# The last stage of a streaming encoder step: where its weights and residual are fetched, and in which order its blocks, sums and outputs run

## The chip, the core and the metric

The kernel runs on one core of a Trainium2 chip. A core has TensorE (PE, matrix products into PSUM), VectorE (DVE), ScalarE (ACT), GpSimd (POOL) and SyncE (SP, whose queue issues the DMAs). The metric is the device time of one execution in microseconds (us), the median of several runs.

## The reference, cut to what matters

An encoder trunk of two layers works on 656 tokens of 1024 channels (16 meta tokens, 512 prompt tokens, 8 x 16 sample tokens), all in float32. In each layer a mixing block adds to the residual, then a gated feed-forward block does; after the second layer the result is normalised. The end of the second layer is what the change touches:

```python
    gate, val = jnp.split(h2 @ p['w_up'].astype(x.dtype), 2, axis=-1)
    gate_c, ffn_new = causal_dwconv(gate, ffn_past, p['ffn_conv_w'], p['ffn_conv_b'])
    x = x + (jax.nn.gelu(gate_c) * val) @ p['w_down'].astype(x.dtype)
...
    y_prompt = rmsnorm(xp, g_final)[:, N_META:]
    y_sample = rmsnorm(xs, g_final)
```

w_up is 1024 x 5632 and w_down 2816 x 1024. The 2816 inner channels are 22 blocks of 128; the 1024 model channels are 8 blocks of 128, called m = 0 to 7 below.

## The kernel before, in words

Channels lie on the 128 partitions and tokens along the free dimension. Every float32 product is made from three matrix products in a reduced format: an operand is split into a high part (a cast on ScalarE) and a low part (operand minus high part, on VectorE), and `mm3` adds high x high, high x low and low x high into the same PSUM tile. So a block of weights can be used when its load (`w_load`, a tile "raw"; there are 4 of them), its cast (`ghi` or `whi`) and its subtraction (`glo` or `wlo`) are done. `weights` issues the three one after another; with its last argument true the two parts go to tiles of the large pool of 57 slots, else to a small pool of 4.

**The feed-forward stage.** The products with w_up are made for pairs of inner blocks by a scheme of seven products (`strassen`), 12 matrix instructions each. One pair takes seven products for its gate and seven for its value; 133 such products run in the last layer, numbered by `nprod`. When a pair is done, its gated values are multiplied on GpSimd (`gv`, L1275 and L1277), and `val_split` splits them into `hi_g` and `lo_g` (L332, L333), the moving operand of the products with w_down. The inner blocks are taken in four parts (`PARTS`: 6, 6, 6 and 4 blocks). The products of the first three parts with w_down run between the seven-product groups (`down`, named `d_dn`): their results are added by GpSimd-issued DMAs onto the residual, which lies in DRAM (`x_scr`, L1306). The list `steps` holds this order; L1340 opens a block in which VectorE and TensorE follow it as written, while the tile scheduler orders ScalarE, GpSimd and the DMA queues. Splits of finished values wait in the list `later`, which gives one up after each product; what is left is emptied at L1361.

**The last stage** (from L1373) does the fourth part, inner blocks 18 to 21, for the last layer. It stands behind that block, so the scheduler orders all engines. The 640 tokens that matter are cut into two chunks, `CF`: 384 and 256 tokens wide. For each chunk it goes over m = 0 to 7: 4 inner blocks x 3 = 12 matrix instructions into one PSUM tile (`d_fin`); VectorE adds the residual block `x` (L1386), which `x_in` has fetched from `x_scr` (L424); ScalarE squares the sum (`sq`, L408) and scales it (`y`, L1390); GpSimd adds the squares up, for m = 7 VectorE (L413). Then `norm_r` sums the squares over the partitions with a matrix product by ones (`np_fin`, L312), takes the root's reciprocal on ScalarE (L313, L314) and refines it on VectorE (L315, L317); each `y` is multiplied by it (L1394; GpSimd for m = 1 and 4, VectorE for the others) and stored. The weights of m = 0 and 1 are fetched ahead of the loop (`WA` = 2), those of m + 2 and the residual of m within the pass m of the first chunk. PSUM has 8 tiles: 3 in one pool (`PD`) and 5 in another (`PB`); `PX` goes round over both.

## Time and profile before

| | us |
|---|---|
| median of 3 runs (lowest to highest) | 1698.6 (1696.43 to 1701.21) |
| the profiled execution: its time | 1697.38 |
| the profiled execution: its span, first to last instruction | 1695.6 |
| PE busy in the span | 1625.4 (96%) |
| DVE busy | 1238.9 (73%) |
| ACT busy | 878.7 (52%) |
| POOL busy | 581.7 (34%) |

The span lies 1.78 us under the time of the same execution. Stretches are given in us from the span's start. The granted clock of TensorE is a share of full speed: it has two levels, 2.4 GHz (1.00) and 1.2 GHz (0.50), and a value between them is a mean over a stretch.

### The profile page before, as it was taken

What the parts mean: (1) busy time and instruction counts of PE and PEld (TensorE: products, weight loads), DVE (VectorE), ACT (ScalarE), POOL (GpSimd) and SP (SyncE); (2) the same over time, 40 slices, a digit from 0 to 9 for tenths busy, and PEclk for the clock granted to TensorE, in tenths of its full rate; (3) what the DMA queues carried; (4) which work ended last, traced back from release to release, by engine and by line L of the source; (5) the groups of instructions that cost most, each with busy time, mean ns of one, the idle gap of its engine ahead of it and who ended that gap; (6) DMA issues with size and microseconds to landing.
All of it is one profiled execution on the core that took longest, in us unless ns stands there. A gap on an engine that the chain in (4) does not pass through costs nothing.

```text
span 1695.6 us, 28745 instructions
## 1 busy us (share of the span) xinstructions
PE 1625.4 (96%) x10772; PEld 1532.0 (90%) x10772; DVE 1238.9 (73%) x2380; ACT 878.7 (52%) x1744; POOL 581.7 (34%) x668
## 2 busy tenths in 40 slices
PE   7999999998999999999999999999999999999985
PEld 6898888898899999999998978789888999999984
DVE  6579985769877767766648898776898767776444
ACT  5656576553545444444445647575454444444343
POOL 0102220008466554553001122100476555554423
PEclk9999999999999999999999999999999999999998
DMA  5236431342145344444612555214411344344442
GB/s 205 90 96 159 115 99 36 112 154 79 50 112 119 100 105 106 102 102 107 221 65 89 128 130 122 67 65 136 144 38 60 95 120 107 101 102 98 119 110 94
DMA packets 75003, 180.56 MB, mean 106 GB/s; under 512 B 12752, under 2 KB 18384, under 8 KB 74864
## 3 DMA queue, kind: packets, MB, share of 16 engines
q1 hardware_dynamic: 62192, 149.36, 27.3%
q0 software_dynamic: 12672, 29.37, 11.1%
q8 instruction: 84, 1.38, 0.3%
q14 instruction: 55, 0.45, 0.1%
HBM read 129.80 MB, written 35.46 MB: 97 GB/s over the span
## 4 chain that ended last, share of the span: by engine, by line
PE 78%; DVE 10%; issue 4%; POOL 3%; ACT 2%; DMA 2%; SPq 0%; DVEq 0%; POOLq 0%; ACTq 0%
PE d_i L374 16%; PE d_dn L374 15%; PE d_v L374 12%; PE d_g L374 12%; PE d_oa L374 5%; PE e_i L374 2%; PE sc L491 2%; DMA x<-x_scr 1%; PE hl L785 1%; PE po L527 1%; PE e_u L374 1%; DVE fh L1066 1%; DVE wlo L361 1%; PE d_ob L374 1%; DVE wlo L968 1%
## 5 line engine op out<-in xcount | busy, mean ns | idle before, releaser
L374 PE MATMUL d_v<-fh,whi 128*128 128x328 f32 (+1 forms) x1120 | 251.6, 312 | 1.4 <-ACT whi L967 1.4
L360 ACT CAST whi<-raw 128x384 fp32r<-128x384 f32 (+2 forms) x243 | 132.5, 548 | 210.1 <-PE d_i L374 75.5
L374 PE MATMUL d_g<-fh,whi 128*128 128x328 f32 (+1 forms) x1008 | 226.5, 312 | 0.3 <-ACT whi L967 0.3
L374 PE MATMUL d_i<-hi_h,whi 128*128 128x328 f32 x672 | 219.0, 326 | 0.0
L374 PE MATMUL d_i<-lo_h,whi 128*128 128x328 f32 x672 | 213.8, 318 | 0.0
L374 PE MATMUL d_i<-hi_h,wlo 128*128 128x328 f32 x672 | 212.8, 317 | 0.0
L374 PE MATMUL d_dn<-hi_g,wlo 128*128 128x328 f32 (+1 forms) x640 | 199.9, 312 | 2.8 <-DVE wlo L361 2.8
L374 PE MATMUL d_dn<-hi_g,whi 128*128 128x328 f32 (+1 forms) x640 | 200.2, 313 | 1.9 <-ACT hi_g L332 1.7
L374 PE MATMUL d_dn<-lo_g,whi 128*128 128x328 f32 (+1 forms) x640 | 200.2, 313 | 1.8 <-DVE lo_g L333 1.8
L361 DVE TENSOR_TENSOR wlo<-raw,whi 128x384 fp32r<-128x384 f32 (+2 forms) x243 | 169.7, 713 | 30.4 <-ACT whi L360 20.5
L374 PEld LDWEIGHTS d_v<-fh,whi 128*128 128x128 f32 x1120 | 189.3, 189 | 1.6 <-ACT whi L967 1.6
L968 DVE TENSOR_TENSOR wlo<-wcb,whi 128x512 fp32r<-128x512 f32 x152 | 129.4, 851 | 75.8 <-ACT whi L967 74.8
L374 PE MATMUL d_v<-fh,wlo 128*128 128x328 f32 (+1 forms) x560 | 175.5, 313 | 3.1 <-DVE wlo L968 3.1
L374 PEld LDWEIGHTS d_g<-fh,whi 128*128 128x128 f32 x1008 | 170.4, 189 | 0.5 <-ACT whi L967 0.5
L374 PE MATMUL d_g<-fh,wlo 128*128 128x328 f32 (+1 forms) x504 | 157.9, 313 | 2.3 <-DVE wlo L968 2.3
L961 POOL TENSOR_TENSOR wcb<-raw 128x512 f32<-128x512 f32 x76 | 111.5, 1468 | 129.2 <-DMA raw<-in_w_up 80.9
L968 DVE TENSOR_TENSOR wlo<-raw,whi 128x512 fp32r<-128x512 f32 x114 | 112.8, 991 | 53.8 <-ACT whi L967 53.5
L967 ACT CAST whi<-wcb 128x512 fp32r<-128x512 f32 x152 | 93.7, 620 | 112.1 <-PE d_g L374 33.3
L374 PEld LDWEIGHTS d_i<-hi_h,whi 128*128 128x128 f32 x672 | 127.1, 189 | 9.6 <-issue 5.2
L374 PEld LDWEIGHTS d_i<-lo_h,whi 128*128 128x128 f32 x672 | 127.3, 189 | 3.8 <-issue 1.3
L374 PEld LDWEIGHTS d_i<-hi_h,wlo 128*128 128x128 f32 x672 | 127.0, 189 | 3.0 <-issue 1.3
L374 PEld LDWEIGHTS d_dn<-hi_g,wlo 128*128 128x128 f32 x640 | 121.1, 189 | 3.5 <-DVE wlo L361 3.5
(385 smaller groups left out, 4053.1 us busy)
## 6 DMA issues: line engine op xcount, KB each, us to landing
raw<-in_w_up SPq DMA_DIRECT2D x88, 512.0 KB, 3.6
raw<-in_w_in SPq DMA_DIRECT2D x45, 512.0 KB, 3.7
raw<-in_w_down SPq DMA_DIRECT2D x48, 384.0 KB, 3.7
x_scr<-x SPq DMA_DIRECT2D x24, 328.0 KB, 3.2
x_scr<-dd POOLq DMA_DIRECT2D x24, 328.0 KB, 4.6
x<-x_scr SPq DMA_DIRECT2D x24, 328.0 KB, 4.3
x_scr<-dd POOLq DMA_DIRECT2D x24, 320.0 KB, 4.5
cvb<-cvt POOLq DMA_DIRECT2D x20, 328.0 KB, 4.9
```

Of the source, the lines that this page charges most:

```text
L360: seq(A.copy(hi[:, :n], raw[:, a:a + n]))
L361: seq(V.tensor_tensor(out=lo[:, :n], in0=raw[:, a:a + n], in1=hi[:, :n].bitcast(F32), op=ALU.subtract))
L374: PE.matmul(ps[:, :b - a], lhsT=ww[:, n], rhs=r[:, a:b], start=first and j == 0, stop=last and j == 2)
L491: PE.matmul(ps[:, o0:o0 + w], lhsT=q[64 * c:64 * c + 64, q0:q0 + 128], rhs=k[64 * c:64 * c + 64, n * w:(n + 1) * w], start=True, stop=True)
L527: PE.matmul(po[:, :128], lhsT=vt[:, j * 128:(j + 1) * 128], rhs=aT[:, j * 128:(j + 1) * 128], start=j == 0, stop=False)
L785: PE.matmul(ps[:, c * 128:(c + 1) * 128], lhsT=kk[:, 16 + 128 * c:144 + 128 * c], rhs=both(m0 + 64 * c, 64), start=True, stop=True)
L961: G.tensor_tensor(out=t, in0=x, in1=y, op=op)
L967: A.copy(hi, x)
L968: V.tensor_tensor(out=lo, in0=x, in1=hi.bitcast(F32), op=ALU.subtract)
L1066: V.tensor_tensor(out=lo, in0=x, in1=hi.bitcast(F32), op=ALU.subtract)
```

## The change

In the last layer the residual blocks 0 to 3 and the weights of blocks 0 to 2 of the last stage are now issued from `steps`, behind products 127 to 133 (`XW`, `WL`). The last stage has a block of its own in which VectorE and TensorE follow the program's order. It begins with the weights of block 3 and with the products of blocks 0 to 3 of the first chunk for the first two of its four inner blocks, into four PSUM tiles side by side (`head`); only then are the last two inner blocks split (`later`), and blocks 4 to 7 of the residual fetched. The loop over m ends those four blocks and makes the other four whole. The squares are added up on VectorE, one pass late (`add_sq`). The first chunk's norm is made within the second chunk's loop (`norm_a` behind m = 1, `norm_b` behind m = 3), and its outputs are multiplied on VectorE behind m = 4 to 7 and after the loop. In the second chunk the last squares are not added on VectorE: the sum over the partitions takes two sources. Its outputs are multiplied two blocks at a time (`finish2`). GpSimd has no work in the last stage.

```diff
@@ -50,7 +50,9 @@
 NE = 7
 WA = 2
 CF = ((16, 400), (400, 656))
-YP = ((1, 4), (1, 4))
+
+XW, WL = {127: (0,), 129: (1,), 131: (2,), 133: (3,)}, {129: (0,), 131: (1,), 132: (2,)}
+YP = (1, 4)
 
 LEVELS = (1, 2, 4, 8, 16, 32, 64)
 KORD = [4, 5, 6, 7, 0, 1, 2, 3]
@@ -313,6 +315,28 @@
             A.activation(out=r[:, a:b], in_=ps[:, :n], func=AF.Abs_reciprocal_sqrt, bias=epsb, scale=1.0)
             A.activation(out=t[:, a:b], in_=r[:, a:b], func=AF.Square)
             V.scalar_tensor_tensor(out=t[:, a:b], in0=ps[:, :n], scalar=EPS, in1=t[:, a:b], op0=ALU.add, op1=ALU.mult)
+        a, b = cc[0][0], cc[-1][1]
+        V.scalar_tensor_tensor(out=r[:, a:b], in0=t[:, a:b], scalar=-3.0, in1=r[:, a:b], op0=ALU.add, op1=ALU.mult)
+        return r
+
+
+    def norm_a(ones, srcs, nm, cc=CA):
+        r = S(f"r_{nm}")
+        t = S(f"rt_{nm}")
+        sums = []
+        for c, (a, b) in enumerate(cc):
+            ps = PB(f"np_{nm}{c}")
+            n = b - a
+            for j, s in enumerate(srcs):
+                PE.matmul(ps[:, :n], lhsT=ones, rhs=s[:, a:b], start=j == 0, stop=j == len(srcs) - 1)
+            A.activation(out=r[:, a:b], in_=ps[:, :n], func=AF.Abs_reciprocal_sqrt, bias=epsb, scale=1.0)
+            A.activation(out=t[:, a:b], in_=r[:, a:b], func=AF.Square)
+            sums.append(ps)
+        return r, t, sums, cc
+
+    def norm_b(r, t, sums, cc):
+        for ps, (a, b) in zip(sums, cc):
+            V.scalar_tensor_tensor(out=t[:, a:b], in0=ps[:, :b - a], scalar=EPS, in1=t[:, a:b], op0=ALU.add, op1=ALU.mult)
         a, b = cc[0][0], cc[-1][1]
         V.scalar_tensor_tensor(out=r[:, a:b], in0=t[:, a:b], scalar=-3.0, in1=r[:, a:b], op0=ALU.add, op1=ALU.mult)
         return r
@@ -1315,7 +1339,7 @@
             return [step(m) for m in range(8)]
 
 
-        steps, nprod = [], 0
+        steps, nprod, wl = [], 0, []
         due = [(a + j * gap, n, j) for n, (a, gap) in enumerate(DOWN[l]) for j in range(8)]
         parts = [down(n) for n in range(3)]
 
@@ -1334,6 +1358,11 @@
                     while due and due[0][0] <= nprod:
                         _, n, j = due.pop(0)
                         steps.append(parts[n][j])
+                    if l == depth - 1:
+                        for m in XW.get(nprod, ()):
+                            steps.append((0, None, None, lambda m=m: x_in(m, xdr)))
+                        for m in WL.get(nprod, ()):
+                            steps.append((0, None, None, lambda m=m: wl.append(weights(wd[m], *PARTS[l][3], True))))
 
 
 
@@ -1358,7 +1387,7 @@
                     later.pop(0)()
             if behind is not None:
                 behind()
-            while later:
+            while later and l < depth - 1:
                 later.pop(0)()
         nc.sync.dma_start(out=o["ffn"][l], in_=gout.rearrange("p f n -> p (f n)"))
         if l < depth - 1:
@@ -1372,28 +1401,75 @@
 
     f0, nf = PARTS[l][3]
     ks = list(range(f0, f0 + nf))
-    wl = [weights(wd[m], f0, nf, True) for m in range(WA)]
-    for c, (a, b) in enumerate(CF):
-        w = b - a
-        nt = 1 if c == 0 else 2
-        ys = []
-        for m in range(8):
-            if c == 0 and m < 8 - WA:
-                wl.append(weights(wd[m + WA], f0, nf, True))
-            if c == 0:
-                x_in(m, xdr)
-            ps = gemm1(wl[m], ks, gts, f"fin{c}{m}", (a, b))
-            V.tensor_tensor(out=xs[m][:, a:b], in0=ps[:, :w], in1=xs[m][:, a:b], op=ALU.add)
-            sq_add(m, (a, b))
-            if m % nt == 0:
-                ys.append(S(f"y{c}{m}")[:, :nt * w].rearrange("p (m n) -> p m n", m=nt))
-            A.activation(out=ys[-1][:, m % nt], in_=xs[m][:, a:b], func=AF.Copy, scale=par("g_fin", m))
-        r = norm_r(onesd[:, 0], [sq_acc["t"]], f"fin{c}", ((a, b),))
-        for m in range(8):
-            y = ys[m // nt]
-            (G if m in YP[c] else V).tensor_tensor(out=y[:, m % nt], in0=y[:, m % nt], in1=r[:, a:b], op=ALU.mult)
-            if m % nt == nt - 1:
-                nc.sync.dma_start(out=o["y"][m + 1 - nt:m + 1, :, a - NM:b - NM].rearrange("m p n -> p m n"), in_=y)
+
+    def finish(m, y, r, nt, a, b, E):
+        E.tensor_tensor(out=y[:, m % nt], in0=y[:, m % nt], in1=r[:, a:b], op=ALU.mult)
+        if m % nt == nt - 1:
+            nc.sync.dma_start(out=o["y"][m + 1 - nt:m + 1, :, a - NM:b - NM].rearrange("m p n -> p m n"), in_=y)
+
+
+    ys, r, sq = ([], []), None, []
+
+    def add_sq(a, b):
+        t, s = sq[0], sq.pop()
+        if sq:
+            V.tensor_tensor(out=t[:, a:b], in0=t[:, a:b], in1=s[:, a:b], op=ALU.add)
+        else:
+            sq.append(s)
+
+    def finish2(m, r, a, b):
+
+        y = ys[1][m]
+        V.tensor_tensor(out=y, in0=y, in1=dims(r[:, a:], (0, 2), (1, b - a)), op=ALU.mult)
+        nc.sync.dma_start(out=o["y"][2 * m:2 * m + 2, :, a - NM:b - NM].rearrange("m p n -> p m n"), in_=y)
+
+    with tc.manual_schedule(engines={mybir.EngineType.DVE, mybir.EngineType.PE}):
+
+        wl.append(weights(wd[3], f0, nf, True))
+        a, b = CF[0]
+        head = [PX(f"d_fin0{m}") for m in range(4)]
+        for m in range(4):
+            for k in range(nf - 2):
+                mm3(head[m], wl[m][k], gts[ks[k]], (a, b), k == 0, False)
+        while later:
+            later.pop(0)()
+        for m in range(4, 8):
+            x_in(m, xdr)
+        for c, (a, b) in enumerate(CF):
+            w = b - a
+            nt = 1 + c
+            for m in range(8):
+                if c == 0 and m < 4:
+                    wl.append(weights(wd[m + 4], f0, nf, True))
+                if c == 0 and m < 4:
+                    ps = head[m]
+                    for k in range(nf - 2, nf):
+                        mm3(ps, wl[m][k], gts[ks[k]], (a, b), False, k == nf - 1)
+                else:
+                    ps = gemm1(wl[m], ks, gts, f"fin{c}{m}", (a, b), PX)
+                V.tensor_tensor(out=xs[m][:, a:b], in0=ps[:, :w], in1=xs[m][:, a:b], op=ALU.add)
+                if m > 1:
+                    add_sq(a, b)
+                elif c == 1 and m == 0:
+                    add_sq(*CF[0])
+                    first = sq.pop()
+                sq.append(S(f"sqf{c}{m}"))
+                A.activation(out=sq[-1][:, a:b], in_=xs[m][:, a:b], func=AF.Square)
+                if m % nt == 0:
+                    ys[c].append(S(f"y{c}{m}")[:, :nt * w].rearrange("p (m n) -> p m n", m=nt))
+                A.activation(out=ys[c][-1][:, m % nt], in_=xs[m][:, a:b], func=AF.Copy, scale=par("g_fin", m))
+                if c == 1 and m == 1:
+                    nrm = norm_a(onesd[:, 0], [first], "fin0", (CF[0],))
+                if c == 1 and m == 3:
+                    r = norm_b(*nrm)
+                if c == 1 and m > 3:
+                    for n in {4: (0, 1), 5: (2, 3), 6: (4,), 7: (5,)}[m]:
+                        finish(n, ys[0][n], r, 1, *CF[0], V)
+        for n in (6, 7):
+            finish(n, ys[0][n], r, 1, *CF[0], V)
+        r = norm_r(onesd[:, 0], sq, "fin1", (CF[1],))
+        for m in range(4):
+            finish2(m, r, *CF[1])
 
 
 def kernel(**inputs):
```

## Rows read from the trace of the kernel before

**Rows 1.** Windows: busy us (and instructions) of each engine, granted clock, DMA share, GB/s.
```profile
1620.00:1637.10 17.10, 17.09 (x116) 16.82 (x115) 8.49 (x15) 6.49 (x12) 4.36 (x4) 1.00 0.40 85
1637.10:1641.56 4.46, 0.00 (x0) 0.00 (x0) 1.66 (x3) 1.92 (x4) 2.50 (x4) 1.00 0.00 0
1641.56:1663.32 21.76, 20.52 (x96) 17.89 (x97) 8.74 (x15) 9.73 (x19) 4.80 (x5) 0.92 0.51 173
...
1676.42:1695.60 19.18, 1.23 (x3) 0.50 (x2) 11.53 (x17) 5.87 (x17) 9.50 (x10) 0.59 0.39 137
```

**Rows 2.** Chain that ended last, from 1639: start, duration, engine, tile, line.
```profile
1639.64 0.73 ACT hi_g L332
...
1643.03 3.33 DMA x<-x_scr
...
1688.55 0.43 DVE y L1394
...
1689.84 1.87 DVE y L1394 x4
```

**Rows 3.** Timeline of PE: start, us, line, operation; in brackets idle before it, releaser.
```profile
1641.56 0.45 PE L374 MATMUL d_fin<-hi_g,ghi 128*128 128x384 f32 x1 [4.47 <-ACT ghi L360]
...
1646.04 0.34 PE L374 MATMUL d_fin<-hi_g,glo 128*128 128x384 f32 x1
...
1652.15 0.34 PE L374 MATMUL d_fin<-lo_g,ghi 128*128 128x384 f32 x1
...
1672.34 0.91 PE L312 MATMUL np_fin<-sq,onesd 128*128 128x384 f32 x2
...
1674.03 0.28 PE L374 MATMUL d_fin<-hi_g,glo 128*128 128x256 f32 x1
...
1676.14 0.28 PE L374 MATMUL d_fin<-hi_g,glo 128*128 128x256 f32 x1
1685.42 1.22 PE L312 MATMUL np_fin<-sq,onesd 128*128 128x256 f32 x2 [8.99 <-DVE sq L413]
```

**Rows 4.** Timeline of DVE in the last stage.
```profile
1640.39 1.56 DVE L333 TENSOR_TENSOR lo_g<-gv,hi_g 128x640 fp32r<-128x640 f32 x2 [2.77 <-ACT hi_g L332]
...
1655.80 0.55 DVE L1386 TENSOR_TENSOR x<-d_fin,x 128x384 f32<-128x384 f32 x1
...
1658.57 0.55 DVE L1386 TENSOR_TENSOR x<-d_fin,x 128x384 f32<-128x384 f32 x1
...
1676.86 0.42 DVE L1386 TENSOR_TENSOR x<-d_fin,x 128x256 f32<-128x256 f32 x1
```

**Rows 5.** Groups by line and shape, 1641 to 1696: busy us, mean ns, idle before.
```profile
L1394 DVE TENSOR_TENSOR y<-y,r_fin 128x384 f32<-128x384 f32 x6 | 6.3, 1120 | 0.0
L413 POOL TENSOR_TENSOR sq<-sq,sq 128x384 f32<-128x384 f32 x6 | 6.1, 1017 | 21.9 <-ACT sq L408 21.9
L361 DVE TENSOR_TENSOR glo<-raw,ghi 128x512 fp32r<-128x512 f32 x8 | 5.4, 690 | 8.0 <-ACT ghi L360 8.0
L1386 DVE TENSOR_TENSOR x<-d_fin,x 128x256 f32<-128x256 f32 x8 | 3.4, 424 | 9.2 <-PE d_fin L374 9.2
L1394 POOL TENSOR_TENSOR y<-y,r_fin 128x384 f32<-128x384 f32 x2 | 2.6, 1309 | 0.0
L413 DVE TENSOR_TENSOR sq<-sq,sq 128x384 f32<-128x384 f32 x1 | 0.5, 548 | 0.0
```

**Rows 6.** Timeline of SP's DMA queue, and one row of GpSimd's.
```profile
829.03 0.32 SPq L420 DMA_DIRECT2D x_scr<-x  x1
829.46 0.37 SPq L424 DMA_DIRECT2D x<-x_scr  x1
...
1626.15 0.33 SPq L343 DMA_DIRECT2D raw<-in_w_down  x1
...
1632.62 0.87 POOL L1306 DMA_DIRECT2D x_scr<-dd  x1 [8.66 <-ACT dd L1305]
...
1642.59 0.33 SPq L343 DMA_DIRECT2D raw<-in_w_down  x1
```

## The prediction

> **What bounds the kernel now.** I read the windows over the end of the run first [rows 1], because the change touches nothing ahead of product 127. Up to 1637.1 TensorE is busy all the time at a granted clock of 1.00, so nothing that merely moves work under those products shows. Then come 4.46 us without a matrix instruction, 21.76 us for the first chunk at a mean clock of 0.92, the second chunk from 1663.32 to 1676.42, and 19.18 us in which TensorE does next to nothing. The gap, the clock and the last stretch are what a reader should look at: of the 58.5 us behind product 133 the matrix work itself needs about half, as the next step shows.
>
> The chain that ended last says what fills the rest [rows 2]. TensorE's gap ends when `hi_g` of the last inner blocks, then the weight casts queued behind it on ScalarE, are there. The first residual block comes 3.33 us after it was issued at 1643.03, since its DMA stood in SP's queue behind a weight load that waited for a free raw tile. At the end the last sum by ones (`np_fin`) starts at 1685.42: TensorE has waited 8.99 us for the square sums, which GpSimd adds up one behind another [rows 3].
>
> TensorE's own timeline gives the rates [rows 3]. In the first chunk 36 instructions start from 1646.04 to 1652.15: 6.11/35 = 0.1746 us each. In the second, 19 start from 1674.03 to 1676.14: 2.11/18 = 0.1172. VectorE's timeline shows why the first chunk is slower than that: from one residual add to the next it takes 1658.57 - 1655.80 = 2.77 us, while the 12 instructions of a block need 12 x 0.1746 = 2.10 [rows 3, 4]. The add, the square, the scaling, the cast of the next weights and their subtraction follow one another.
>
> **The change, part by part.**
>
> *Products.* Before, TensorE needs from 1637.09 (the 4.47 us gap counted back from 1641.56) to 1676.42: 39.33 us [rows 1, 3]. After, the head can start as soon as product 133 ends: it needs inner blocks 18 and 19, whose splits were put on `later` behind product 126, and weights that are fetched behind products 129 to 132. Both chunks then are 96 x 0.1746 + 96 x 0.1172 = 16.76 + 11.25 = 28.0 us, and the first norm's sum is put between the products as before, 0.91 us: 28.9 in all. If TensorE never waits, that is 39.3 - 28.9 = **10.4 us** less. Inside it are the gap and most of the lower clock that followed it (the mean of 0.92 in the next window): the head's 24 instructions are 4.2 us long and fill it.
>
> *Does the head find its weights?* The raw tiles free themselves as before: the fourth load of the last stage was issued at 1626.15 already [rows 6], 11 us ahead of the head, and lay unused until about 1641. What came late was the cast and the subtraction, 0.69 us on VectorE per block [rows 5]. Now three of the four are written between the products, where VectorE is busy 8.49 of 17.1 us and ScalarE 6.49 [rows 1]; 3 x 0.69 = 2.1 us more fit. I cost this at nothing. Without that cover, every split that is not ready would hold VectorE, and behind it the products' results in PSUM.
>
> *What is late next.* The head ends at 1637.0 + 4.2 = 1641.1. Then it needs `hi_g` and `lo_g` of the last two inner blocks. Those are bound by GpSimd's products, and end before as now: `hi_g` from 1639.64 [rows 2], the two `lo_g` from 1640.39 to 1641.95 [rows 4]. The second is wanted some four instructions after 1641.1, so at 1641.8: a wait of 0.1 us. One thing is new there. The split of weight block 3 runs on VectorE at about 1637.6, beside GpSimd's last gate products. The trace shows what two inputs from SBUF on both engines cost: a y product of 384 columns took 1120 ns on VectorE beside GpSimd's sums, a square sum of that size alone 548, and on GpSimd 1309 (beside VectorE) against 1017 [rows 5]. GpSimd's product of the last block has 640 columns, 1.7 us at 1017 for 384; stretched by 1309/1017 it makes `hi_g` up to 0.5 us late. I take 0.4 for both, with bounds of 0 and 1. (The Trainium skill, GPSIMD Engine Reference, section Specifications, says that GpSimd's SBUF interfaces are shared with VectorE and contended by VectorE instructions with two SBUF inputs. The trace agrees: 1120 against 548 ns. By the rule this split is paid in full and the sum below would be 17.4; were it free, 17.9.)
>
> *The tail.* Before, from the last product's end at 1676.42 to the end of the span: 19.18 us [rows 1]. After, in order: the add starts 0.44 us behind the product, as before (1676.86) [rows 4]. VectorE may be behind by then. In the second chunk a block takes TensorE 1.41 us; VectorE has two operations of 0.42 and, at m = 3, 4 and 5, two more of 384 columns at 0.55: 1.94 by whole durations, so up to 3 x 0.53 = 1.6 of backlog. But neighbours overlap: six y products of 1120 ns are busy 6.3 us and not 6.7, 0.08 each [rows 5]; with that, and with what m = 6 and 7 give back, it is 0.1. I take 0.9. Then the add 0.42, the square as much (0.42), and the sum by ones over two sources: one source took 1.22 at the lower clock after 8.99 idle, and 0.91 x 256/384 = 0.61 at the full one [rows 3]. TensorE has now been idle for 2 us only, so I take twice 0.61 = 1.2 (bounds 0.6 and 2.5). The root and its refinement: from 1686.64 to 1688.55, 1.9 [rows 2, 3]. Four output products of two blocks, 512 columns, at the 0.69 of a subtraction of that size, 0.08 of it overlapped: 2.5. The two first-chunk outputs behind the loop, 1.1 us of VectorE, lie under the square, the sum and the root. From the last output product to the end: 1695.6 - 1691.71 = 3.9 [rows 2], unchanged, since the last stores are as large as before. Sum: 0.4 + 0.9 + 0.4 + 0.4 + 1.2 + 1.9 + 2.5 + 3.9 = 11.6, so **7.6 us** less. What goes is GpSimd's chain of sums and ScalarE's late squares; the output products of the first chunk, 6.3 us on VectorE behind the last product [rows 5], now run under the second chunk and at 0.55 each. The norm of the first chunk stands between squares on ScalarE still, but with work left on TensorE behind it.
>
> *DMAs.* The eight residual fetches and weight loads are the same in number. Blocks 0 to 3 now pass SP's queue ahead of the last weight loads; a fetch has nothing to wait for but the additions into its own block. That the queue doesn't wait for other blocks is seen at the end of layer 0: a store of one block at 829.03 is followed by the fetch of the next at 829.46 [rows 6]. At 40% DMA share they fit [rows 1]. Cost nothing.
>
> Sum: 10.4 + 7.6 - 0.4 = 17.6. The profiled execution took 1697.38, 1.78 of it outside the span; 1697.4 - 17.6 = 1679.8. It lies 1.2 below the median of the runs, 1698.6, so the median after should be **1681**.
>
> **Rivals.**
>
> *The block cycle stays.* ScalarE isn't in given order. If it does a block's square and scaling ahead of the next weight cast, and VectorE, now in order, waits for that cast ahead of the next add, the first chunk goes on at 2.77 a block: 8 x 2.77 - 16.8 = 5.4 lost, 1686. For it: the row of 2.77. Against: the head leaves four blocks only half to do, so TensorE has 8 us of products whose weights are ready, and four weights, not six, are split in the loop.
>
> *SP's queue holds.* If a fetch placed behind product 131 waits for the last addition (issued from 1632.62 to 1633.5 [rows 6]; by the 3.33 of a fetch, landed at 1636.8) and weight block 3 stands behind it, its load lands at 1640.1 and its split ends 1.4 later, at 1641.5; the two `lo_g` stand behind it and end at 1643.1, not 1641.95, and the head's fourth block waits as well: some 2 us, 1683.
>
> *The tail stays.* The edit may not do what it says: the scheduler may again put the first chunk's root on ScalarE ahead of the second chunk's squares. Then only the products' 10.4 - 0.4 are won: 1688.5. Against: the squares' sums are in order now and follow TensorE, and the root is ready while six blocks are still to come.
>
> *Slower.* VectorE in given order stands at a weight split whose load isn't there; product results queue behind it, PSUM's eight tiles fill and TensorE stops. An unready split costs at most a landing of 3.33 and 0.69 twice, 4.7 us. To be slower by over 0.3% (5 us, about what a measurement of this kernel tells from no change) it has to eat 22.6 us: five of the eight splits fully late. Against it stands the load at 1626.15 [rows 6]. (The Trainium skill, TensorE: Matmul & The Clock Gate, section Architectural detail, calls ScalarE's and VectorE's queues strictly first in, first out: what stands behind the split can't pass. No run here shows it by itself.)
>
> **How the numbers follow.** Forecast (1677 to 1685) 0.68; block cycle 0.13; SP's queue 0.06; tail stays 0.07; a mixture that wins less than 5 us 0.03; slower 0.03. Low end: no backlog, no wait for `hi_g`, one source of the sum hidden: 0.9 + 0.4 + 0.6 = 1.9 less, and the scatter of the runs (2 us below their median): 1677. High end: the block cycle and SP's queue are inside, the tail half: 1688. Faster by over 0.3%: 0.94, within it 0.03, slower 0.03.
>
> **What would show it.** The head: no idle time above 1 us on TensorE behind product 133 and a granted clock of 1.00 through the first chunk. The loop: adds 2.1 us or less apart from m = 4 on. The products end near 1666, the span near 1678. The tail: under 12 us from the last product to the end, np_fin at about 0.6 us a source, y products near 0.55. Wrong would be: VectorE waiting for ScalarE's `ghi` for microseconds between products 129 and 133 (slower or queue), ScalarE's squares of the second chunk behind its root (tail stays), adds 2.8 us apart with TensorE idle (block cycle).

## The result, and the profile after

The changed kernel takes 1678.91 us (median of 5 runs, 1678.5 to 1682.5), the kernel before 1698.6 (5 runs beside it, 1695.18 to 1701.4): a ratio of 0.9896, 95% interval 0.9881 to 0.991. The profiled execution of the changed kernel has a span of 1677.1 us, 18.5 less than before. Lines of the changed kernel stand 24 or more further down; L398 is the matrix product (L374 before), L385 the weights' subtraction (L361).

Windows of the changed kernel, cut at the ends of product 133, of the first chunk's sums and of the last product (columns as in [rows 1]):

```profile
1619.00:1636.02 17.02, 17.02 (x117) 17.02 (x116) 10.54 (x19) 8.51 (x16) 4.31 (x4) 1.00 0.60 146
1636.02:1654.50 18.48, 17.82 (x101) 16.99 (x101) 11.45 (x20) 9.41 (x19) 3.43 (x4) 1.00 0.38 129
1654.50:1666.11 11.61, 11.61 (x96) 11.14 (x94) 8.64 (x22) 8.83 (x19) 0.00 (x0) 1.00 0.10 35
1666.11:1677.10 10.99, 1.13 (x4) 0.68 (x4) 6.25 (x14) 2.52 (x6) 0.00 (x0) 0.75 0.58 203
```

The 4.46 us without a matrix instruction [rows 1] are gone, the clock is 1.00 through both chunks, and the stretch behind the last product is 10.99 us where it was 19.18. TensorE's timeline shows the seam:

```profile
1635.70 0.32 PE L398 MATMUL d_v<-fh,wlo 128*128 128x322 f32 x1
1635.85 0.34 PE L398 MATMUL d_fin<-hi_g,ghi 128*128 128x384 f32 x1
...
1639.88 0.34 PE L398 MATMUL d_fin<-hi_g,glo 128*128 128x384 f32 x1
1640.45 0.44 PE L398 MATMUL d_fin<-hi_g,ghi 128*128 128x384 f32 x1 [0.24 <-ACT hi_g L356]
1641.31 0.45 PE L398 MATMUL d_fin<-lo_g,ghi 128*128 128x384 f32 x1 [0.42 <-DVE lo_g L357]
1641.59 0.34 PE L398 MATMUL d_fin<-hi_g,glo 128*128 128x384 f32 x1
1641.77 0.34 PE L398 MATMUL d_fin<-hi_g,ghi 128*128 128x384 f32 x1
1642.05 0.45 PE L398 MATMUL d_fin<-lo_g,ghi 128*128 128x384 f32 x1
1642.33 0.33 PE L398 MATMUL d_fin<-hi_g,glo 128*128 128x384 f32 x1
...
1665.84 0.27 PE L398 MATMUL d_fin<-hi_g,glo 128*128 128x256 f32 x1
1667.66 1.13 PE L314 MATMUL np_fin<-sqf,onesd 128*128 128x256 f32 x4 [1.55 <-DVE sqf L1416]
```

The head starts under the last instruction of product 133 and runs without a hole to 1639.88. Then the next six starts, up to 1642.33, take 2.45 us where six take 1.05 at the rate of 0.175 [rows 3]: 1.4 us are lost to `hi_g` and `lo_g`. Nothing else stops TensorE before 1666.11. VectorE's timeline:

```profile
1642.70 0.56 DVE L1450 TENSOR_TENSOR x<-d_fin,x 128x384 f32<-128x384 f32 x1
...
1645.47 0.55 DVE L1450 TENSOR_TENSOR x<-d_fin,x 128x384 f32<-128x384 f32 x1
...
1648.24 0.55 DVE L1450 TENSOR_TENSOR x<-d_fin,x 128x384 f32<-128x384 f32 x1
...
1651.01 0.55 DVE L1450 TENSOR_TENSOR x<-d_fin,x 128x384 f32<-128x384 f32 x1
...
1651.94 0.55 DVE L1450 TENSOR_TENSOR x<-d_fin,x 128x384 f32<-128x384 f32 x1
...
1666.86 0.41 DVE L1450 TENSOR_TENSOR x<-d_fin,x 128x256 f32<-128x256 f32 x1
...
1670.70 2.50 DVE L1423 TENSOR_TENSOR y<-y,r_fin 128x512 f32<-128x512 f32 x4
```

The first four adds are still 2.77 us apart, as before [rows 4]; from m = 4 on they follow 0.93 apart, until VectorE has caught up with TensorE. Of the groups, the output products of the first chunk answer to the 1120 ns of [rows 5]:

```profile
L1406 DVE TENSOR_TENSOR y<-y,r_fin 128x384 f32<-128x384 f32 x8 | 4.1, 550 | 0.0
```

For a sum that the scatter of whole runs doesn't blur, I count the stage from the end of product 133 (the last `d_v` instruction of TensorE's timeline) to the end of the span, and cut it at the end of the last product (`d_fin`); the two parts are called products and tail below. The end of product 133 itself lies between 1634.85 and 1640.93 in the 14 profiles of this study, for reasons far ahead of the change: from a DMA that GpSimd issues at 1324.72 (1323.68 in the changed kernel) to the end of product 133 it is 312.34 to 312.37 us in all of them. So the fetches and splits between the products cost nothing ahead of the stage. The changed kernel's comes 1.07 us earlier than before's (1636.02 against 1637.09), so of its 18.5 us 17.43 belong to the stage.

| kernel | stage | products | tail | median | ratio to before (95%) |
|---|---|---|---|---|---|
| before | 58.51 | 39.33 | 19.18 | 1698.6 | |
| changed | 41.08 | 30.09 | 10.99 | 1678.91 | 0.9896 (0.9881 to 0.991) |
| no_head | 45.37 | 34.38 | 10.99 | 1686.1 | 0.9932 (0.9912 to 0.9952) |
| weights_late | 41.39 | 30.35 | 11.04 | 1680.68 | 0.9907 (0.9892 to 0.9922) |
| resid_late | 41.18 | 30.19 | 10.99 | 1679.13 | 0.9895 (0.9878 to 0.9911) |
| weights_sooner | 40.16 | 29.12 | 11.04 | 1678.32 | 0.9895 (0.9878 to 0.9912) |
| fetch_none | 41.13 | 30.14 | 10.99 | 1680.03 | 0.9901 (0.9886 to 0.9916) |
| fetch_alone | 50.89 | 31.71 | 19.18 | 1689.24 | 0.9948 (0.9932 to 0.9964) |
| sums_on_gpsimd | 41.25 | 31.04 | 10.21 | 1680.04 | 0.9898 (0.9879 to 0.9918) |
| first_outputs_last | 41.87 | 30.08 | 11.79 | 1680.43 | 0.9896 (0.9879 to 0.9913) |
| free_order | 40.75 | 30.09 | 10.66 | 1679.48 | 0.9891 (0.9871 to 0.991) |
| resid_first_alone | 52.04 | 40.41 | 11.63 | 1691.1 | 0.9965 (0.9953 to 0.9978) |
| norm_in_loop_alone | 57.31 | 39.24 | 18.07 | 1696.02 | 0.9991 (0.998 to 1.0003) |
| sooner_free | 39.74 | 29.15 | 10.59 | 1681.08 | 0.9907 (0.9891 to 0.9923) |

The first three columns come from one profiled execution each. A variant of the changed kernel within 2 us of it can be told from it by the stage only: its runs scatter by more. Of the edits below nine are made to the changed kernel; fetch_alone, resid_first_alone and norm_in_loop_alone are made to the kernel before and do one part of the change.

### The profile page after: what moved, and what is told of

It reads as the page before. It is cut to its first block, busy times and chain, and to the rows that moved or that the text cites. A ratio compares the mean times of both kernels' runs of the same rounds, so it can differ in the third digit from the quotient of the medians.

```text
span 1677.1 us, 28733 instructions
## 1 busy us (share of the span) xinstructions
PE 1618.5 (97%) x10774; PEld 1527.1 (91%) x10774; DVE 1245.9 (74%) x2391; ACT 879.1 (52%) x1744; POOL 566.8 (34%) x652
## 4 chain that ended last, share of the span: by engine, by line
PE 78%; DVE 11%; issue 4%; POOL 3%; ACT 2%; DMA 1%; SPq 0%; POOLq 0%; DVEq 0%; ACTq 0%
PE d_dn L398 16%; PE d_i L398 16%; PE d_v L398 12%; PE d_g L398 12%; PE d_oa L398 5%; PE sc L515 2%; PE e_i L398 1%; PE hl L809 1%; PE po L551 1%; DVE fh L1090 1%; DVE wlo L385 1%; PE d_fin L398 1%; PE e_u L398 1%; DVE wlo L992 1%; POOL gv L1299 1%
## 5 line engine op out<-in xcount | busy, mean ns | idle before, releaser
L398 PE MATMUL d_v<-fh,whi 128*128 128x328 f32 (+1 forms) x1120 | 251.8, 312 | 1.6 <-ACT whi L991 1.6
L398 PE MATMUL d_g<-fh,whi 128*128 128x328 f32 (+1 forms) x1008 | 226.5, 312 | 0.3 <-ACT whi L991 0.3
L398 PE MATMUL d_i<-hi_h,whi 128*128 128x328 f32 x672 | 219.3, 326 | 0.0
L398 PE MATMUL d_i<-lo_h,whi 128*128 128x328 f32 x672 | 213.9, 318 | 0.0
L398 PE MATMUL d_i<-hi_h,wlo 128*128 128x328 f32 x672 | 212.9, 317 | 0.0
L398 PE MATMUL d_dn<-hi_g,wlo 128*128 128x328 f32 (+1 forms) x640 | 199.8, 312 | 2.8 <-DVE wlo L385 2.8
L398 PE MATMUL d_dn<-hi_g,whi 128*128 128x328 f32 (+1 forms) x640 | 200.2, 313 | 1.9 <-ACT hi_g L356 1.7
L398 PE MATMUL d_dn<-lo_g,whi 128*128 128x328 f32 (+1 forms) x640 | 200.1, 313 | 1.8 <-DVE lo_g L357 1.8
L385 DVE TENSOR_TENSOR wlo<-raw,whi 128x384 fp32r<-128x384 f32 (+2 forms) x243 | 170.9, 717 | 30.5 <-ACT whi L384 22.7
L398 PEld LDWEIGHTS d_v<-fh,whi 128*128 128x128 f32 x1120 | 189.3, 189 | 2.2 <-ACT whi L991 2.2
L398 PE MATMUL d_v<-fh,wlo 128*128 128x328 f32 (+1 forms) x560 | 175.5, 313 | 3.3 <-DVE wlo L992 3.3
L398 PEld LDWEIGHTS d_g<-fh,whi 128*128 128x128 f32 x1008 | 170.4, 189 | 0.5 <-ACT whi L991 0.5
L398 PE MATMUL d_g<-fh,wlo 128*128 128x328 f32 (+1 forms) x504 | 157.8, 313 | 2.3 <-DVE wlo L992 2.3
L398 PEld LDWEIGHTS d_i<-hi_h,whi 128*128 128x128 f32 x672 | 127.5, 190 | 10.1 <-issue 5.6
L398 PEld LDWEIGHTS d_i<-lo_h,whi 128*128 128x128 f32 x672 | 127.6, 190 | 3.8 <-issue 1.3
L398 PEld LDWEIGHTS d_i<-hi_h,wlo 128*128 128x128 f32 x672 | 127.2, 189 | 3.0 <-issue 1.3
L398 PEld LDWEIGHTS d_dn<-hi_g,wlo 128*128 128x128 f32 x640 | 121.1, 189 | 3.5 <-DVE wlo L385 3.5
```

Source lines behind the costliest of these rows:

```text
L385: seq(V.tensor_tensor(out=lo[:, :n], in0=raw[:, a:a + n], in1=hi[:, :n].bitcast(F32), op=ALU.subtract))
L398: PE.matmul(ps[:, :b - a], lhsT=ww[:, n], rhs=r[:, a:b], start=first and j == 0, stop=last and j == 2)
```

## The experiments

**The head left out** (no_head). The products go block by block, four inner blocks at a time:

```diff
-        head = [PX(f"d_fin0{m}") for m in range(4)]
-        for m in range(4):
-            for k in range(nf - 2):
-                mm3(head[m], wl[m][k], gts[ks[k]], (a, b), k == 0, False)
...
-                if c == 0 and m < 4:
-                    ps = head[m]
-                    for k in range(nf - 2, nf):
-                        mm3(ps, wl[m][k], gts[ks[k]], (a, b), False, k == nf - 1)
-                else:
-                    ps = gemm1(wl[m], ks, gts, f"fin{c}{m}", (a, b), PX)
+                ps = gemm1(wl[m], ks, gts, f"fin{c}{m}", (a, b), PX)
```

> The changed kernel without its head: the last two inner blocks are split first, then all eight blocks of the first chunk are made whole, one after another; early fetches, order and tail stay. The changed kernel takes 41.1 us from the end of product 133 to the end of the span (before: 58.5). Theory (the head fills the wait for the last inner blocks and keeps the clock up): TensorE stands some 4 us behind product 133 and then runs a stretch at the lower clock, 46.5 us, +5.5 on the whole. Rival (early fetch and given order bring the gain, the head only moves products): 42 us, under +1.

The stage grew by 4.29 us, all of it products; 5.5 were expected. TensorE's timeline of no_head, behind six instructions of the first block:

```profile
1645.31 0.45 PE L398 MATMUL d_fin<-hi_g,ghi 128*128 128x384 f32 x1 [3.34 <-ACT hi_g L356]
...
1647.94 0.53 PE L398 MATMUL d_fin<-hi_g,ghi 128*128 128x384 f32 x1
1648.26 0.53 PE L398 MATMUL d_fin<-lo_g,ghi 128*128 128x384 f32 x1
```

The gap is back, and behind it the instructions start 0.32 us apart, not 0.175; the granted clock from 1645.31 to 1649.20 is 0.57. So with the rest of the change in place the head is worth 4.3 of the 9.2 us by which the products got shorter.

**Weights as late as before** (weights_late). Blocks 0 to 2 are fetched and split where block 3 is:

```diff
-... {129: (0,), 131: (1,), 132: (2,)}
+... {}
-        wl.append(weights(wd[3], f0, nf, True))
+        for m in range(4):
+            wl.append(weights(wd[m], f0, nf, True))
```

> The weights of blocks 0 to 2 are no longer loaded, cast and split between products 129 and 132 but with block 3's behind product 133; the residual stays early. Theory (the loads are in their raw tiles anyway, only the splits move): the head starts some 2 us later, but VectorE has no split beside GpSimd's last gate products, so the last inner blocks come about 1 us sooner: +0.5 to +1.5, some 42 us from product 133 to the end. Rival (the early fetch of the weights is what fills the gap): +4 or more.

Only 0.3 us longer, under the range that was expected, and not for its reason. GpSimd and VectorE in weights_late, where product 133 ends at 1637.51:

```profile
1638.37 0.90 POOL L1301 TENSOR_TENSOR gv<-gv,ga 128x128 f32<-128x128 f32 x1
1639.23 1.74 POOL L1299 TENSOR_TENSOR gv<-gv,ga 128x512 f32<-128x512 f32 x1
```

```profile
1637.55 0.49 DVE L1018 TENSOR_TENSOR gv<-d_v,us_v 128x322 f32<-128x322 f32 x1 [0.29 <-PE d_v L398]
1637.96 1.86 DVE L385 TENSOR_TENSOR glo<-raw,ghi 128x512 fp32r<-128x512 f32 x2
```

The splits still meet GpSimd's gate products, now behind the result of product 133, and `hi_g` starts 3.89 us behind that product (1641.40) against 3.65 in the changed kernel (1639.67).

**The residual late** (resid_late). `XW = {}`, and blocks 0 to 3 are fetched with 4 to 7, behind the head:

```diff
-        for m in range(4, 8):
+        for m in range(8):
             x_in(m, xdr)
```

> Residual blocks 0 to 3 are fetched with 4 to 7, behind the head; the weights stay early. Theory: the first block lands some 3 us after VectorE wants it, then the adds follow at 2.77 us a block because each waits for the next weight split; TensorE has products for about 8 us and then waits for the weights of blocks 6 and 7: +2 (1 to 4). Rival (hidden by the head and by eight PSUM tiles): 0.

This expectation failed: 0.1 us. SP's queue and VectorE in resid_late, where product 133 ends at 1638.92:

```profile
1640.85 4.20 SPq L448 DMA_DIRECT2D x<-x_scr  x8
```

```profile
1645.61 0.56 DVE L1450 TENSOR_TENSOR x<-d_fin,x 128x384 f32<-128x384 f32 x1
```

The first add comes 6.69 us behind product 133, and 6.68 in the changed kernel (1642.70 - 1636.02). With a landing of 3.33 us [rows 2] a fetch issued at 1640.85 is there at about 1644.2 by estimate, before anyone asks for it. With the head there, the early fetch has nothing left to hide.

**Neither is fetched early** (fetch_none): both edits in one.

> The changed kernel with neither weights nor residual issued between products 127 and 133: all are written at the head of the last stage. Theory (each of the two alone cost under 0.4 us, the scheduler draws the weight splits forward by itself): +0 to +1, 41 to 42 us from product 133 to the end. Rival (one covered for the other): +3 or more.

The stage is 41.13, the changed kernel's but for 0.05. So in the presence of the head and the new order, the part of the change that its description puts first, the fetches between the products, is worth nothing that shows. VectorE's timeline of fetch_none says why:

```profile
1632.96 1.28 DVE L385 TENSOR_TENSOR glo<-raw,ghi 128x512 fp32r<-128x512 f32 x2
...
1635.14 2.38 DVE L385 TENSOR_TENSOR glo<-raw,ghi 128x512 fp32r<-128x512 f32 x2
1637.45 0.48 DVE L1018 TENSOR_TENSOR gv<-d_v,us_v 128x322 f32<-128x322 f32 x1
```

All four splits are written behind product 133, and all four stand ahead of its result at 1637.45: the scheduler drew them forward. So the given order of one block of the program doesn't keep a later block's instructions behind it. In the kernel before the casts stood behind `hi_g` (1639.64 [rows 2]) on ScalarE:

```profile
1640.89 1.66 ACT L360 CAST ghi<-raw 128x512 fp32r<-128x512 f32 x3
```

There `hi_g` is written ahead of them, now behind the head. That this is what let the casts go forward is a reading; no run changes it alone.

**Blocks 1 to 3 split sooner** (weights_sooner): blocks 1 and 2 one product sooner, block 3 behind product 131 and not at the head.

```diff
-... {129: (0,), 131: (1,), 132: (2,)}
+... {129: (0,), 130: (1,), 131: (2, 3)}
-        wl.append(weights(wd[3], f0, nf, True))
```

> The weights of blocks 0 to 3 are split behind products 129, 130, 131 and 131 instead of 129, 131, 132 and the head's beginning, so that no split runs on VectorE beside GpSimd's last gate products. Theory (the split of block 2, 2.38 us for two where one alone takes 0.69, holds the last product's result and stretches GpSimd): the high part of the last inner blocks 1.1 us sooner, TensorE's waits behind the head down from 1.3 to 0.2 us: -1.1. Rival (GpSimd's own products set that time): 0.

0.92 us shorter, all of it products (29.12). GpSimd and VectorE in the changed kernel:

```profile
1635.31 1.61 POOL L1299 TENSOR_TENSOR gv<-gv,ga 128x512 f32<-128x512 f32 x1 [2.90 <-issue]
1636.88 0.88 POOL L1301 TENSOR_TENSOR gv<-gv,ga 128x128 f32<-128x128 f32 x1
1637.94 1.29 POOL L1299 TENSOR_TENSOR gv<-gv,ga 128x512 f32<-128x512 f32 x1 [0.18 <-DVE gv L1018]
```

```profile
1635.08 2.38 DVE L385 TENSOR_TENSOR glo<-raw,ghi 128x512 fp32r<-128x512 f32 x2
1637.39 0.48 DVE L1018 TENSOR_TENSOR gv<-d_v,us_v 128x322 f32<-128x322 f32 x1
```

and in weights_sooner:

```profile
1636.33 1.29 POOL L1299 TENSOR_TENSOR gv<-gv,ga 128x512 f32<-128x512 f32 x1 [2.91 <-DVE gv L1018]
1637.58 0.44 POOL L1301 TENSOR_TENSOR gv<-gv,ga 128x128 f32<-128x128 f32 x1
1637.98 1.29 POOL L1299 TENSOR_TENSOR gv<-gv,ga 128x512 f32<-128x512 f32 x1
```

```profile
1633.91 1.29 DVE L385 TENSOR_TENSOR glo<-raw,ghi 128x512 fp32r<-128x512 f32 x2
1635.29 0.49 DVE L1022 TENSOR_TENSOR us_v<-d_v,us_v 128x322 f32<-128x322 f32 x1
...
1637.07 0.49 DVE L1018 TENSOR_TENSOR gv<-d_v,us_v 128x322 f32<-128x322 f32 x1 [0.89 <-PE d_v L398]
```

In the changed kernel two splits meet GpSimd's gate product and take 2.38 us, not 1.29. The result of product 133, done at 1636.02, stands behind them until 1637.39, and GpSimd's last product starts 1.92 us behind product 133. In weights_sooner the splits are over before GpSimd starts; the result goes 0.03 us behind product 133 (1637.04), the last GpSimd product 0.94. That is the 1 us, and TensorE's wait behind the head shrinks with it, from 1.4 us to 0.4. Two delays run side by side here: the result held on VectorE, done 1.85 us behind product 133 (1637.87), and GpSimd's own last product but one, stretched and done 1.74 behind it (1637.76). In weights_late the result isn't held, and the last GpSimd product still starts 1.72 us behind product 133 (1639.23 - 1637.51). So GpSimd's stretch alone makes most of the delay.

**The early fetches alone** (fetch_alone): the kernel before with the change's `XW` and `WL`; the loop fetches blocks 3 to 7 of the weights and 4 to 7 of the residual, and nothing else is changed:

```diff
+                    if l == depth - 1:
+                        for m in XW.get(nprod, ()):
+                            steps.append((0, None, None, lambda m=m: x_in(m, xdr)))
+                        for m in WL.get(nprod, ()):
+                            steps.append((0, None, None, lambda m=m: wl.append(weights(wd[m], *PARTS[l][3], True))))
...
-            if c == 0 and m < 8 - WA:
-                wl.append(weights(wd[m + WA], f0, nf, True))
-            if c == 0:
+            if c == 0 and m < 5:
+                wl.append(weights(wd[m + 3], f0, nf, True))
+            if c == 0 and m > 3:
                 x_in(m, xdr)
```

> The kernel before with one thing of the change: residual blocks 0 to 3 and weights 0 to 2 issued between products 127 and 133. Theory (the rest of the products' time is the gap that only the head fills, and the tail is untouched): 3 to 6 us of the 58.5 go, the tail stays at 18 to 19 us. Rival (the fetches are the change): 12 or more.

The products took 31.71, 7.6 us less than before: more than expected, and most of what the whole change brings there. The tail is 19.18, before's to the hundredth. TensorE in fetch_alone, product 133 ending at 1636.41:

```profile
1638.16 0.34 PE L375 MATMUL d_fin<-hi_g,glo 128*128 128x384 f32 x1
1640.14 0.79 PE L375 MATMUL d_fin<-hi_g,ghi 128*128 128x384 f32 x3 [1.64 <-ACT hi_g L333]
```

With early split weights at hand the scheduler places 12 instructions of two blocks behind product 133, half a head, by itself, and 1.64 us of gap are left. The edit moves weights and residual; since the residual alone, fetched ahead of the loop, leaves the gap at 4.48 us (resid_first_alone), it is the weights that close it. So early splits and a head in the program's text are two ways to much the same gain: of the 9.2 us of products each alone brings most (9.2 in fetch_none, 7.6 in fetch_alone), and the two don't add up.

**The squares' sums back on GpSimd** (sums_on_gpsimd), still one pass late:

```diff
-            V.tensor_tensor(out=t[:, a:b], in0=t[:, a:b], in1=s[:, a:b], op=ALU.add)
+            G.tensor_tensor(out=t[:, a:b], in0=t[:, a:b], in1=s[:, a:b], op=ALU.add)
```

> The changed kernel with its square sums (13 additions) on GpSimd, as before; all else stays. Theory (what was lost before was the order, GpSimd's chain itself keeps up at 0.9 us a block against 1.41 of TensorE; but GpSimd's additions stretch VectorE's outputs of the first chunk from 0.55 to about 1.1): VectorE wins 6 x 0.42 and loses up to 6 x 0.5 in the second chunk, the last addition is 0.9 and not 0.42: +0.5 to +2. Rival (GpSimd's chain is what made the tail long): +5 or more.

The tail became shorter, 10.21; TensorE waited 0.7 us for the first chunk's sum instead, and the stage is 0.17 longer, less than the 0.5 to 2 expected. GpSimd's last sum in that kernel:

```profile
1665.75 0.73 POOL L1416 TENSOR_TENSOR sqf<-sqf,sqf 128x256 f32<-128x256 f32 x1 [0.39 <-ACT sqf L1457]
```

It ends at 1666.48, while the products end at 1665.89. GpSimd's chain of sums, which the prediction blamed for the old tail, keeps up once the squares come in time (it has no output products between its sums here).

**The first chunk's outputs behind the loop** (first_outputs_last):

```diff
-                if c == 1 and m > 3:
-                    for n in {4: (0, 1), 5: (2, 3), 6: (4,), 7: (5,)}[m]:
-                        finish(n, ys[0][n], r, 1, *CF[0], V)
-        for n in (6, 7):
+        for n in range(8):
```

> The eight outputs of the first chunk are multiplied behind the second chunk's loop instead of within it (six) and behind it (two). Theory (VectorE has a backlog of only 0.3 us in the loop and the two behind it are hidden; six more of 0.47 make 3.8 us of which 2.5 lie under square, sum and root): +1.0 to +1.5, tail from the last product 12 to 12.5 us instead of 11.0. Rival (where they run does not matter): 0; other rival (all of them come on top): +2.8.

The eight take 3.83 us from 1667.23 on, the root's refinement waits for them (ready at 1669.46, started at 1670.98), and the tail grows by 0.8, a little less than expected.

**The scheduler's order** (free_order). The second block no longer gives VectorE and TensorE their order:

```diff
-    with tc.manual_schedule(engines={mybir.EngineType.DVE, mybir.EngineType.PE}):
+    if True:
```

> The last stage with the scheduler's order on VectorE and TensorE instead of the given one; head, fetches and tail are the same instructions. Theory (the gain comes from what runs where and when it is fetched; the given order is worth little): -0.5 to +1.5. Rival (given order brings it): +5 or more.

0.33 us shorter, in the tail. With the rest of the change in place the given order isn't needed for the short tail.

**The residual ahead of the loop, alone** (resid_first_alone): the kernel before with one edit.

```diff
+    for m in range(8):
+        x_in(m, xdr)
     for c, (a, b) in enumerate(CF):
...
-            if c == 0:
-                x_in(m, xdr)
```

> The kernel before with one edit: all eight residual blocks are fetched ahead of the first chunk's loop, not one in each pass. Theory (before, the scheduler put the first chunk's last residual add behind four adds of the second chunk on VectorE, so the first norm, ScalarE's root and with it all squares of the second chunk came 7 us late; fetched up front the adds keep their order): the tail falls from 19.2 to 12 to 15 us with sums on GpSimd, norm between the chunks and no given order; the products' 39.3 us stay within 2. Rival (GpSimd's sums, or the norm's place, make the tail): it stays at 18 to 19.

The tail fell from 19.18 to 11.63, a little further than expected; the products took 40.41, 1.1 more: the second chunk is 1.9 us longer, since six y products (5.79 us from 1670.88) now stand ahead of its adds on VectorE and TensorE waits 2.3 us for adds. The whole stage is 6.5 us shorter. Here is what the edit did. The kernel before, on VectorE and on ScalarE (a row of x2 joins neighbours of one line and prints the first one's shape):

```profile
1661.34 0.55 DVE L1386 TENSOR_TENSOR x<-d_fin,x 128x384 f32<-128x384 f32 x1
1664.94 0.89 DVE L1386 TENSOR_TENSOR x<-d_fin,x 128x256 f32<-128x256 f32 x2 [3.05 <-PE d_fin L374]
...
1669.99 0.89 DVE L1386 TENSOR_TENSOR x<-d_fin,x 128x256 f32<-128x256 f32 x2 [0.99 <-PE d_fin L374]
```

```profile
1665.91 0.52 ACT L408 ACTIVATE sq<-x 128x384 f32<-128x384 f32 x1 [2.96 <-PE d_fin L374]
...
1670.96 0.52 ACT L408 ACTIVATE sq<-x 128x384 f32<-128x384 f32 x1 [4.02 <-PE d_fin L374]
...
1675.66 0.40 ACT L408 ACTIVATE sq<-x 128x256 f32<-128x256 f32 x1
```

and resid_first_alone:

```profile
1661.88 0.56 DVE L1386 TENSOR_TENSOR x<-d_fin,x 128x384 f32<-128x384 f32 x1 [0.96 <-PE d_fin L374]
1663.99 0.56 DVE L1386 TENSOR_TENSOR x<-d_fin,x 128x384 f32<-128x384 f32 x1 [1.55 <-PE d_fin L374]
```

```profile
1669.13 0.40 ACT L408 ACTIVATE sq<-x 128x256 f32<-128x256 f32 x1
```

Before, the first chunk's last product was done at 1663.49, but its add stands in VectorE's queue behind that of the second chunk's m = 3: the second of the two at 1669.99, whose square of 384 columns follows at 1670.96. So the first norm's sum starts 8.85 us behind that product (1672.34 [rows 3]), and behind its root on ScalarE stand all eight squares of the second chunk: from 1675.66 on, when all but the last of their products are done. GpSimd adds them up only then, with two output products (2.58 us) among the sums, until 1684.91. With the residual fetched ahead, the add comes at 1663.99, 0.04 us behind its product (1663.95), the norm's sum 1.86 us behind it (1665.81), the second chunk's squares start at 1669.13, and the tail is 7.55 us shorter. The residual itself was not late before: its last fetch was issued by 1652.53. It is the place in the queue that moved with the place of the fetch; that the scheduler places an add by when it reckons its residual to land is my reading, and no trace shows the reckoning.

**The norm within the loop, alone** (norm_in_loop_alone): the kernel before with `norm_a` behind m = 1 and `norm_b` and the outputs behind m = 3 of the second chunk.

```diff
-        r = norm_r(onesd[:, 0], [sq_acc["t"]], f"fin{c}", ((a, b),))
...
+            if c == 1 and m == 1:
+                nrm = norm_a(onesd[:, 0], [first], "fin0", (CF[0],))
+            if c == 1 and m == 3:
+                outs(0, y0, norm_b(*nrm))
```

> The kernel before with the first chunk's norm written within the second chunk's loop, as in the change; sums, order and fetches stay as before. Theory (the late residual add rules): tail 18 to 19 us as before, products 39 us. Rival (the norm's place makes the tail): 11 to 13 us.

The tail stayed at 18.07, and the ratio's interval holds 1. The adds stand as before:

```profile
1670.89 0.89 DVE L1417 TENSOR_TENSOR x<-d_fin,x 128x256 f32<-128x256 f32 x2 [1.00 <-PE d_fin L395]
```

**Both small gains together** (sooner_free): weights_sooner and free_order.

> The changed kernel with the weights of blocks 0 to 3 split behind products 129, 130, 131 and 131, and the last stage in the scheduler's order. Theory (the two edits, -0.9 and -0.3 us of the 41.1 alone, act in different places): 39.8 us from product 133 to the end. Rival (they take from the same wait): 40.2 to 40.8.

The stage is 39.74 us, 1.34 under the changed kernel's, as the two add up to (0.92 + 0.33 = 1.25). The median, 1681.08, is not lower: product 133 ended at 1640.56 in its profile, and what such an edit moves ahead of the stage, or what merely scatters there, is larger than it wins. I can't call it a faster kernel.

## Why the prediction came out right, and where its steps were off

**The sum.** 17.6 us were predicted for the stage, 17.43 measured; the other 1.07 of the span's 18.5 came from ahead of the stage and were not foreseen. The median, 1678.91, lies 2.1 under the predicted 1681: these 1.07, and 1.2 that were added for a profiled execution below its median, while here the profiled execution is the median. (The text gives the high end twice, 1685 in the forecast and 1688 in its working; the result lies under both.) Two terms were off, products by 0.8 and tail by 0.6, in opposite directions; that the sum came out to 0.2 us is luck.

**Products: 29.3 predicted (28.9 and the wait of 0.4), 30.09 measured.** The rates held: both chunks at the clock of 1.00 and no other wait. The mis-sized term is the wait for `hi_g` and `lo_g` behind the head: 1.4 us measured, over the upper bound of 1 (the first norm's sum took about 0.66 between the products and not 0.91). The place was right, a weight split beside GpSimd's last gate products. But the prediction let one split meet the last GpSimd product and stretched it by 1309/1017, 0.5 us at most. Two splits met the last but one, which ended 0.76 us later behind product 133 than in weights_sooner (1.74 against 0.98). Besides, the result of product 133 stands behind these splits on VectorE for 1.37 us (1636.02 to 1637.39). (The Trainium skill, TensorE: Matmul & The Clock Gate, section Architectural detail, has VectorE's queue strictly first in, first out; the trace agrees, with these 1.37 us.) By weights_late the stretch alone would make GpSimd's last product nearly as late. weights_sooner removes both, and the stage gives back 0.92.

**What fills the gap.** The prediction had it from the early splits and the head together. The runs are finer: either does most of it, since the scheduler makes half a head when splits are there (fetch_alone, 7.6 of the 9.2 us), and draws the splits forward when a head is there (fetch_none, all 9.2). The costs put at nothing were right: beside the head, weights and residual between the products cost and bring nothing by their place (0.3, 0.1 and 0.05 us), but for the one meeting with GpSimd.

**Tail: 11.6 predicted, 10.99 measured; the size right, the cause not.** In order: from the last product's end to the add 0.75 (0.44 + 0.9 predicted, so a backlog of 0.31 and not 0.9); add and square to 1667.72, 0.86 (0.84); the sum to 1668.79, 1.07 (1.2); the root 1.91 (1.9); four output products 2.50 (2.5); to the end 3.90 (3.9). But "what goes is GpSimd's chain of sums and ScalarE's late squares" was half of it. The squares were late, as said; GpSimd's chain was late behind them, and with the sums on GpSimd the tail of the changed kernel is no longer (10.21). The first link, unseen in the prediction, was VectorE's queue: two adds of the first chunk behind adds of the second, the last one over 6.5 us after its product. In the kernel before neither the norm's new place (18.07) nor the early fetches of blocks 0 to 3 (19.18) remove it; the fetch of all residual blocks ahead of the loop does (11.63). The changed kernel has that too, and its tail stays short without the given order (10.66). Whether the given order alone, on which the prediction relied, would do as much with the fetches left in the loop wasn't tried; so it isn't shown which of the two shortened the tail of the changed kernel.

**The rivals.** *The block cycle* came about: adds 2.77 us apart for m = 0 to 3. It cost nothing, as the argument against it said: four blocks were half done, PSUM held what followed, and at the last add of the chunk VectorE was 0.57 us behind TensorE (1654.74 against 1654.17). *SP's queue* wasn't held up: the loads are issued by 1637.9 and TensorE never waits for a weight. *The tail stays* did not happen. *Slower*: a split did hold VectorE, with product 133's result behind it, for the 1.37 us above and not for the 22.6 it needed.

## What to carry to other kernels

When a stall has a long chain behind it, look at each engine's queue for the first instruction that ran late although its operands were there; here a residual add 6.5 us behind its product moved a whole norm, and moving the residual's fetches was worth 7.5 us of tail (6.5 of the stage). Two edits that feed the same gap (early splits, products that need less) don't add up: try each without the other before crediting either. And a fill-in operation placed between products is free only where it doesn't meet another engine's work on the way to the next wait.

## What the runs showed of the hardware that was not expected

Two VectorE subtractions of 512 columns took 2.38 us beside two GpSimd products, 1.29 without; GpSimd's took 1.61 and 0.88, 1.29 and 0.44 without. The starts fit taking turns better than sharing: GpSimd's first is longer by 0.32, about what VectorE's first has left when it starts (by its usual 0.69: 1635.77 - 1635.31 = 0.46), its second by 0.44, and VectorE's two by 1.09, close to a whole GpSimd product. In fetch_alone a single split begins 0.22 us ahead of GpSimd's first product (1635.47 and 1635.69); it takes 0.68 as alone, and only GpSimd's is longer, 1.61. (The Trainium skill, SBUF — State Buffer, section Who interferes with whom, calls the port pair of the two engines an exclusive lock; these rows agree.) So a short operation of two inputs on VectorE can, by these rows, be late by nearly the other engine's whole instruction, and what stands behind it as well.
